# The second down-projection of a decoder trunk by seven block products

## The chip, the cores and the metric

The kernel runs on one core of one Trainium2 chip. The metric is the device time of one execution in microseconds; what is given as the time of the kernel is the median of several runs. Beside the runs there is one execution taken with the hardware profiler, and all rows below come from that one.

## The reference

The program is a decoder trunk of two layers on 1024 tokens of 1024 channels, in float32. The first layer mixes with a gated short convolution and differential attention, the second with RWKV-7 time mixing. After each mixer stands a channel mixer (FFN), and it is the second FFN that the change is about:

```python
def conv_glu_ffn(x, w_up, conv_w, conv_b, w_down):
    h = causal_dwconv(x @ w_up, conv_w) + conv_b
    gate, up = jnp.split(h, 2, axis=-1)
    return (jax.nn.silu(gate) * up) @ w_down
...
        f = conv_glu_ffn(x, ffn_w_up[l], ffn_conv_w[l], ffn_conv_b[l], ffn_w_down[l])
        x = layer_norm(DN_ALPHA * x + f, ln2_g[l], ln2_b[l])
```

The inner width is 2816, so `w_up` is 1024 x 5632 and `w_down` 2816 x 1024. The convolution reaches two tokens back.

## The kernel before

**Precision.** Every large product is made of three matmuls (`mm3`, lines 135 to 139): each operand is split into a rounded high part and the remainder in float32r, and high x high, high x low and low x high are summed in PSUM. `split` (line 113) makes the parts: a cast on ScalarE (L114) and a subtraction on VectorE (L115).

**The FFN.** `ffn` (line 215) is a generator that is called once for each layer `l`. The 2816 inner channels are `NC` = 22 chunks of 128. For each chunk `c` the up-projection makes a gate and a value tile, channels by 1024 tokens. Seven block products already stand in place of eight there (a Winograd form of Strassen's scheme): the 2 x 2 blocks are the gate and value weights by the two halves of the 1024 inputs, and the tokens' two halves. `block` (line 230) loads a chunk's weights with two transfers of 512 KB (`wr<-wup`, L236, on SP's queue) and makes the sums S1 to S4 on VectorE (L246). `cast` and `sub` (L254, L261) split a block five products ahead. From chunk 2 on, `chained` (line 358) emits one product of 12 matmuls (four input blocks by three passes) and then the other engines' work; the order of the products in a chunk is 1, 6, 2, 5, 7, 3, 4. Bank reads between products are `u` L366 and L376, `hv` L379 to L385 and `gi` L383. `late` (line 329) spreads the convolution, the gate and the loads of chunk `c` over the products of chunk `c + 1`: at product 1 it calls for S1 of the chunk after, at product 7 it multiplies gate and value (L353) and stores the tile in DRAM as `G` (L354, on POOL's queue).

**The down-projection.** `operands` (line 397) loads a chunk's half of `G` (256 KB, SP) and its 128 x 1024 rows of `wdn` (512 KB, SP) and splits both; `down` (line 421) multiplies them into PSUM. Tokens go in two groups of 512. In a group each of four token tiles has two banks (1024 output columns), and all 22 chunks are summed into them: 2 groups x 22 chunks x 4 token tiles x 2 column halves x 3 passes are 1056 matmuls. At the end of a group the last chunks (six in the last group) are taken one token tile at a time, so that adding the residual, the statistics, the normalization and the store of a tile run beside the matmuls of the next (`tail`, L489 to L498).

**Order.** The program is written in one sequence and a scheduler makes each engine's queue from it: an engine takes the first instruction in the text whose inputs and buffers are free. From chunk 2 on, the up-projection stands in a region (`manual_schedule`) in which the engines of `ORDERED`, that is TensorE, VectorE and ScalarE, keep the order of the text; SP, which issues the loads, and POOL are not among them. Buffers: `U` is a pool of 40 tiles of 512 KB, `W` of 6 and `RAW` of 2; a chunk's first weight tile is in `RAW`, its second in `U`. A load of the second FFN's weights is queued on SP behind the load of the next chunk's `RAW` tile, which waits for the sum S4 that last reads the tile before.

Of the kernel before, what the change touches and what calls it, by code (L numbers as in the profile page):

```python
# [16 lines left out]
P = 128  # L17
T = 1024
# [18 lines left out]
SUMS = 6  # L37
FIRST = (1, 2, 3, 5, 6, 7, 4)
# [22 lines left out]
class Kern:  # L61
# [153 lines left out]
    def ffn(self, l, xo, resid, row, tail, nxt=None):  # L215
# [7 lines left out]
        GS = [self.pd.tile([P, T], F32, name=f"G{l}_{c}") for c in range(NC)]  # L223
# [70 lines left out]
        def value(c):  # L294
            w = W[c]
            v = conv(w["h"], NC + c)
            nc.vector.tensor_tensor(v, w["g"], v, op=ALU.mult)
            nc.gpsimd.dma_start(GS[c], v)
            w.clear()
# [28 lines left out]
        def late(c, i):  # L328

            b = c - 1  # L330
            if i == 5 and c < NC:
                w = W[c]
                w["gi"] = self.U("gi")
                nc.scalar.copy(w["gi"][:, lo], w["x"])
            if i == 4:
                w = W[c]
                w["g"] = self.U("cv")
                tap(w["g"], w["gi"], c, 0)
            if b > 1:
# [46 lines left out]

        seq = [(c, i) for i in FIRST for c in range(2)]
# [15 lines left out]
        with ExitStack() as region:  # L403
            for n, (c, i) in enumerate(seq):
# [7 lines left out]
                if n == len(seq) - 3:  # L412
                    operands(0, 0)
                    operands(0, 1)
                yield
            for i in (1, 6, 2, 5, 7):
# [1141 lines left out]
def build(tc, ins, out, stop=None):  # L1558
    with ExitStack() as ctx:
# [18 lines left out]
        def mixed(i, l, w, resid, alpha, out_args, last_tail, nxt=None):  # L1578

            tail, res = k.make_tail(f"l{i}g", f"l{i}b", None, "hl")  # L1580
            gen = k.ffn(l, res["xo"], res["spill"], row(i), last_tail, nxt)
# [129 lines left out]
```

## Time and profile before

| | |
|---|---|
| median of 3 runs | 2765.36 us (2763.47 to 2773.1) |
| profiled execution, its own time | 2769.9 us |
| span of its instructions | 2768.1 us |
| TensorE matmuls, busy share of the span | 94% |
| VectorE | 70% |
| ScalarE | 41% |
| POOL (GpSimd) | 10% |
| mean granted TensorE clock | 0.958 of full speed |
| DMA | 358 MB, 129 GB/s in the mean |

A busy share is that of the engine's instructions over the span. Matmuls are pipelined: the profile gives 0.39 us to one, but they start 0.23 us apart, so costs are taken from counts over a stretch. An engine's idle time is listed with what ended it. The stages of interest: the first up-projection with its up matmuls from 533 to 971 us (the first of them between those of the mixer), the first down-projection to 1215, the second up-projection from 2081 to 2520, the second down-projection to 2758.

### The profile page before, as it was taken

Reading aid. Unit: us, or ns where it says so; the run is one execution under the profiler, and the core shown is the slowest. Engines: PE = TensorE matmul, PEld = TensorE weight load, DVE = VectorE, ACT = ScalarE, POOL = GpSimd, SP = SyncE. Lnnn points to the kernel's source line nnn. Section 1 sums busy time; section 2 is a strip of 40 time slices with the busy share of each in tenths; the row PEclk is TensorE's granted clock in tenths of the full one; section 3 lists DMA queues with packets and bytes.
Section 4 is the critical chain, followed back from the end, with each engine's and each line's share of the span. In section 5 each row is a group of like instructions: output and inputs, shape, how many; then the busy total and the mean of one; then the engine's idle time right before and its main releaser. Section 6 shows DMA issues by size and latency. Waiting matters only on the chain. (4 is left out here: it accounts for less than half of the span.)

```text
span 2768.1 us, 37639 instructions
## 1 busy us (share of the span) xinstructions
PE 2596.0 (94%) x14736; PEld 2133.1 (77%) x14736; DVE 1937.0 (70%) x3013; ACT 1123.2 (41%) x1706; POOL 275.4 (10%) x247
## 2 busy tenths in 40 slices
PE   8999989989999999999997988688898999999998
PEld 6777778778888888877876766677776888888887
DVE  4655655598888865667778656786758888887673
ACT  3333332344444441426676223333425444444330
POOL 0000000100000003010011011343420000000000
PEclk9999999999999999999998999887999999999999
DMA  5111223212222273633256678786441222225660
GB/s 168 54 46 44 73 88 110 85 61 92 76 84 92 73 264 117 218 128 114 91 183 236 221 219 234 182 195 171 174 147 46 94 82 92 76 84 184 230 217 31
DMA packets 208674, 358.07 MB, mean 129 GB/s; under 512 B 88944, under 2 KB 118256, under 8 KB 208496
## 3 DMA queue, kind: packets, MB, share of 16 engines
q1 hardware_dynamic: 198704, 320.01, 36.5%
q0 software_dynamic: 9792, 35.66, 3.4%
q8 instruction: 116, 1.90, 0.3%
q14 instruction: 62, 0.51, 0.1%
HBM read 255.46 MB, written 95.94 MB: 127 GB/s over the span
## 5 line engine op out<-in xcount | busy, mean ns | idle before, releaser
L137 PE MATMUL up<-x,wu 128*128 128x512 f32 x1232 | 481.8, 393 | 18.5 <-DVE u L312 8.2
L138 PE MATMUL up<-x,wu 128*128 128x512 f32 x1232 | 482.9, 392 | 0.3 <-DVE x L145 0.2
L139 PE MATMUL up<-x,wu 128*128 128x512 f32 x1232 | 482.0, 391 | 0.0
L137 PEld LDWEIGHTS up<-x,wu 128*128 128x128 f32 x1232 | 232.8, 189 | 71.0 <-ACT x L144 14.4
L138 PE MATMUL dn<-wdl,gt 128*128 128x512 f32 x704 | 273.7, 389 | 0.0
L137 PE MATMUL dn<-wdh,gt 128*128 128x512 f32 x704 | 272.2, 389 | 0.3 <-ACT xf L179 0.3
L139 PE MATMUL dn<-wdh,gt 128*128 128x512 f32 x704 | 272.3, 389 | 0.0
L138 PEld LDWEIGHTS up<-x,wu 128*128 128x128 f32 x1232 | 233.1, 189 | 50.7 <-DVE x L145 2.7
L139 PEld LDWEIGHTS up<-x,wu 128*128 128x128 f32 x1232 | 233.0, 189 | 48.7
L254 ACT CAST wu<-ws 128x512 fp32r<-128x512 f32 x176 | 109.3, 623 | 288.4 <-PE up L139 198.8
L137 PE MATMUL pr<-xv,wph 128*128 128x512 f32 x384 | 154.0, 405 | 9.7 <-DVE kp L1156 7.7
L137 PE MATMUL pj<-x,wih 128*128 128x512 f32 x384 | 153.1, 409 | 7.5 <-ACT x L144 7.5
L115 DVE TENSOR_TENSOR wdl<-raw,wdh 128x1024 fp32r<-128x1024 f32 x88 | 109.7, 1246 | 68.7 <-ACT wdh L114 55.5
L138 PE MATMUL pr<-xv,wph 128*128 128x512 f32 x384 | 153.9, 401 | 3.5 <-DVE xv L915 3.5
L139 PE MATMUL pr<-xv,wpl 128*128 128x512 f32 x384 | 154.2, 402 | 2.6 <-DVE wpl L115 2.6
L139 PE MATMUL pj<-x,wil 128*128 128x512 f32 x384 | 153.8, 401 | 0.2 <-DVE wil L115 0.2
L138 PE MATMUL pj<-x,wih 128*128 128x512 f32 x384 | 153.8, 400 | 0.0
L137 PEld LDWEIGHTS dn<-wdh,gt 128*128 128x128 f32 x704 | 132.2, 188 | 27.8 <-ACT xf L179 0.5
L138 PEld LDWEIGHTS dn<-wdl,gt 128*128 128x128 f32 x704 | 132.2, 188 | 27.7 <-DVE wdl L115 0.3
L139 PEld LDWEIGHTS dn<-wdh,gt 128*128 128x128 f32 x704 | 132.2, 188 | 27.3
L114 ACT CAST wdh<-raw 128x1024 fp32r<-128x1024 f32 x88 | 92.6, 1052 | 108.6 <-DMA raw<-wdn 103.5
L254 ACT CAST wu<-wr 128x512 fp32r<-128x512 f32 x132 | 81.4, 623 | 125.1 <-PE up L139 62.8
(319 smaller groups left out, 5230.8 us busy)
## 6 DMA issues: line engine op xcount, KB each, us to landing
wr<-wup SPq DMA_DIRECT2D x88, 512.0 KB, 4.2
raw<-wdn SPq DMA_DIRECT2D x88, 512.0 KB, 4.2
G<-cv POOLq DMA_DIRECT2D x44, 512.0 KB, 2.9
gr<-G SPq DMA_DIRECT2D x88, 256.0 KB, 4.1
bk<-bkS SPq DMA_DIRECT2D x32, 512.0 KB, 5.9
res<-spill SPq DMA_DIRECT2D x24, 512.0 KB, 4.6
raw<-win SPq DMA_DIRECT2D x22, 512.0 KB, 3.7
spill<-res SPq DMA_DIRECT2D x16, 512.0 KB, 2.8
```

What stands on the lines that cost most here:

```text
L114: self.nc.scalar.copy(hi, raw)
L115: self.nc.vector.tensor_sub(lo, raw, hi.bitcast(F32))
L137: nc.tensor.matmul(ps, ah, bh, start=first, stop=False, **kw)
L138: nc.tensor.matmul(ps, ah, bl, start=False, stop=False, **kw)
L139: nc.tensor.matmul(ps, al, bh, start=False, stop=last, **kw)
L254: nc.scalar.copy(t[:, lo], src)
```

## The change

The second down-projection (`fast`, layer 1 alone) becomes seven block products. With the even chunks and the odd chunks as the two halves of the inner dimension, the left operand A is `G` (token half by chunk parity) and the right operand B is `w_down` (chunk parity by column half). One term of such a product is a *slot*: one pair of chunks `m` (11 of them), 512 tokens by 512 columns, 12 matmuls. Seven products of 11 slots are 77 slots.

The sums of blocks are not made by an engine but by transfers that add to their target in DRAM (`accum_op`), which only POOL's queue issues. The weight sums T1 to T4 (`weight_sums`) are in the text of the first up-projection, at every odd chunk. The sums of `G`, S1 to S4, are made where a chunk is stored (`store`) in the second up-projection: 4 transfers for an even chunk, 7 for an odd one, in place of one each. [...] In the down-projection (`blocks`) SP loads the two operands of a slot (2 x 256 KB), both are split, and the products run in the order `DOWN` over three sets of four banks; residual, block adds, statistics and output are a list of small works, of which each slot takes a portion (`step`). The last chunk's convolution is put into the same list.

```diff
+DOWN = (1, 6, 2, 5, 3, 7, 4)
+WHEN = (4, 7, 10, 13, 18, 21, 24, 27)
...
-        GS = [self.pd.tile([P, T], F32, name=f"G{l}_{c}") for c in range(NC)]
+        fast = l == 1
...
+        def weight_sums(m):
+            t = self.TS[m]
+            b = {f"B{i}{j}": wdn[l + 1, 2 * m + i - 1, :, j * 512 - 512:j * 512] for i in (1, 2) for j in (1, 2)}
+            put = nc.gpsimd.dma_start
+            for n, x in (("T1", "B11"), ("T3", "B12"), ("T2", "B11"), ("T4", "B21")):
+                put(t[n], b[x])
+            for n, x in (("T1", b["B12"]), ("T3", b["B22"]), ("T2", t["T3"]), ("T4", t["T2"])):
+                put(t[n], x, accum_op=ALU.add, max_dma_last_dim=512)
+
+        def store(c, g, v):
+            if not fast:
+                nc.vector.tensor_tensor(v, g, v, op=ALU.mult)
+                nc.gpsimd.dma_start(GS[c], v)
+                return
+            s, put = SS[c // 2], nc.gpsimd.dma_start
+            for h in (lo, hi):
+                if (h is hi) == (c % 2 == 1):
+                    nc.vector.scalar_tensor_tensor(v[:, h], g[:, h], -1.0, v[:, h], ALU.mult, ALU.mult)
+                else:
+                    nc.vector.tensor_tensor(v[:, h], g[:, h], v[:, h], op=ALU.mult)
+            if c % 2 == 0:
+                put(s["S3"], v[:, hi])
+                put(s["N11"], v[:, lo])
+                put(s["S1"], v[:, hi])
+                put(s["S3"], v[:, lo], accum_op=ALU.add)
+            else:
+                put(s["S2"], v[:, hi])
+                put(s["S4"], v[:, lo])
+                put(s["A12"], v[:, lo])
+                put(s["N22"], v[:, hi])
+                put(s["S1"], v[:, hi], accum_op=ALU.add)
+                put(s["S2"], s["S3"], accum_op=ALU.add, max_dma_last_dim=512)
+                put(s["S4"], s["S2"], accum_op=ALU.add, max_dma_last_dim=512)
...
-                    nc.vector.tensor_tensor(w["v"], w["g"], w["v"], op=ALU.mult)
-                    nc.gpsimd.dma_start(GS[b], w["v"])
+                    store(b, w["g"], w["v"])
...
+        terms = {1: ("N11", "B11"), 6: ("S2", "T2"), 2: ("A12", "B21"), 5: ("S1", "T1"), 3: ("S4", "B22"), 7: ("S3", "T3"), 4: ("N22", "T4")}
+        slots = [(i, m) for i in DOWN for m in range(NC // 2)]
...
+        def bring(k):
+            i, m = slots[k]
+            a, b = terms[i]
+            t = raws[k] = self.W("dr", F32)
+            nc.sync.dma_start(t[:, lo], SS[m][a])
+            nc.sync.dma_start(t[:, hi], self.TS[m][b] if b[0] == "T" else wdn[l, 2 * m + int(b[1]) - 1, :, int(b[2]) * 512 - 512:int(b[2]) * 512])
...
+            def finished(i, t):
+                a, b = rs[t], rs[4 + t]
+                if i == 1:
+                    nc.scalar.copy(at(us, t), X[t])
+                elif i == 6:
+                    later(put, at(u2, t), at(us, t), Y[t], front=True)
+                elif i == 2:
+                    later(put, a[:, lo], a[:, lo], X[t], ALU.subtract)
...
+                elif i == 4:
+                    put(b[:, lo], b[:, lo], Z[t], ALU.subtract)
+                    halves(4 + t, 0)
+                    norm(4 + t)
+                    for v in (lo, hi):
+                        later(out, 4 + t, v, cost=1.4, after=1)
...
+            def step():
+                n = tick[0]
+                tick[0] += 1
+                ahead = 5 if n < 6 * 11 - 8 else 9
+                for _ in range(2):
+                    if ready[1] < min(len(slots), n + 1 + ahead):
+                        if ready[0] <= ready[1]:
+                            bring(ready[0])
+                            ready[0] += 1
+                        split_slot(ready[1])
+                        ready[1] += 1
+                    if n < 4:
+                        break
+                while ready[0] < min(len(slots), ready[1] + 3):
+                    bring(ready[0])
+                    ready[0] += 1
...
+            for p, i in enumerate(DOWN):
...
+                ps = X if i in (1, 2) else Z if i in (7, 4) else Y
+                n = NC // 2
+                first = 3 if i in (3, 4) else 1
+                last = 7 if i == 4 else 3 if i in (5, 7) else 1
+                groups = [range(first)] + [range(m, m + 1) for m in range(first, n - last)] + [range(n - last, n)]
+                for g in groups:
+                    for t in range(4):
+                        for m in g:
+                            h, w = parts[p * n + m]
+                            tk = slice(t * P, t * P + P)
+                            self.mm3(ps[t], h[:, tk], w[:, tk], h[:, hi], w[:, hi], m == 0 and i in (1, 6, 7), m == n - 1, skip_group_check=True)
+                            mms[0] += 3
+                            if mms[0] % 12 == 0:
+                                step()
+                        if g[-1] == n - 1:
+                            finished(i, t)
...
+                if n > 14 and i == 3 and not fast:
+                    for m in (0, 1) if c == 3 else (c // 2,) if c % 2 else ():
+                        weight_sums(m)
+                if fast:
+                    if n >= len(seq) - 4:
+                        bring(n - len(seq) + 4)
+                    if n >= len(seq) - 2:
+                        split_slot(n - len(seq) + 2)
+                elif n == len(seq) - 3:
```

## Rows read from the trace of the kernel before

**Rows 1.** Windows: stretch, its length, busy us (instructions) by engine, clock, DMA share, GB/s

```profile
600.00:800.00 200.00, 200.00 (x884) 165.58 (x883) 166.33 (x223) 92.47 (x126) 6.64 (x12) 1.00 0.25 88
...
2200.00:2400.00 200.00, 199.06 (x878) 164.22 (x877) 166.26 (x221) 91.75 (x126) 5.33 (x10) 1.00 0.22 79
...
2500.00:2600.00 100.00, 100.00 (x443) 82.84 (x442) 69.31 (x74) 45.07 (x57) 3.16 (x4) 1.00 0.69 236
```

**Rows 2.** Tiles `up` and `dn`: duration ns min/median/max, first and last start in us

```profile
L139 PE MATMUL up<-x,wu x1232: 387/389/632, 534.0 to 2519.8; 128*128 128x512 f32 x176
...
L139 PE MATMUL dn<-wdh,gt x704: 388/389/397, 971.5 to 2758.3; 128*128 128x512 f32 x176
```

**Rows 3.** Waits, 2150 to 2520 us: us in total, times, longest

```profile
DVE ws L246 <- DMA wr<-wup: 32.5, 18, 3.3
...
PE up L137 <- DVE u L376: 0.9, 2, 0.8
```

**Rows 4.** Timeline of the second up-projection: start, us, instruction [idle before <-releaser]

```profile
2229.51 0.69 DVE L383 TENSOR_TENSOR gi<-u,up 128x512 f32<-128x512 f32 x1 [0.75 <-PE up L139]
2236.30 0.69 DVE L246 TENSOR_TENSOR ws<-wr 128x512 f32<-128x512 f32 x1 [1.58 <-DMA wr<-wup]
2248.55 0.69 DVE L383 TENSOR_TENSOR gi<-u,up 128x512 f32<-128x512 f32 x1 [0.82 <-PE up L139]
2256.42 0.69 DVE L246 TENSOR_TENSOR ws<-wr 128x512 f32<-128x512 f32 x1 [2.66 <-DMA wr<-wup]
2259.56 0.50 PE L137 MATMUL up<-x,wu 128*128 128x512 f32 x1 [0.17 <-DVE u L376]
```

**Rows 5.** DMA in 2229.5:2237 (40 slices; queue: packets, MB, share), then 2248.5:2256.5

```profile
DMA  6000000000000004977985899798989820000000
...
q1 hardware_dynamic: 288, 1.05, 41.0%
...
q1 hardware_dynamic: 288, 1.05, 41.4%
...
q8 instruction: 1, 0.02, 0.9%
```

**Rows 6.** Groups by line, 2500 to 2768 us: shapes, count, busy us, mean ns

```profile
L115 DVE TENSOR_TENSOR wdl<-raw,wdh 128x1024 fp32r<-128x1024 f32 x44 | 53.8, 1223 | 36.6 <-ACT wdh L114 28.7 <-issue 3.6 <-PE dn L138 2.9
L471 DVE TENSOR_TENSOR res<-res,dn 128x512 f32<-128x512 f32 x16 | 10.9, 683 | 45.1 <-PE dn L139 45.1
L496 DVE SCALAR_TENSOR_TENSOR res<-res,mv,bc 128x512 f32<-128x512 f32 x16 | 11.2, 744 | 0.0
...
L114 ACT CAST wdh<-raw 128x1024 fp32r<-128x1024 f32 x44 | 46.3, 1052 | 53.0 <-DMA raw<-wdn 51.1 <-PE dn L138 1.7
```

**Rows 7.** Timeline of POOL's issues in the second layer

```profile
1789.51 0.76 POOL L1467 DMA_DIRECT2D gt<-gateS  x1
...
2246.21 0.53 POOL L354 DMA_DIRECT2D G<-cv  x1 [18.42 <-DVE cv L353]
```

**Rows 8.** DMA of the span: queue 0; issues with KB each and median us to landing

```profile
q0 software_dynamic: 9792, 35.66, 3.4%
...
G<-cv POOLq DMA_DIRECT2D x44, 512.0 KB, 2.9
...
raw<-xT SPq DMA_DIRECT2D x8, 512.0 KB, 3.5
```

**Rows 9.** Timeline of POOL and of SP's queue at the start

```profile
0.73 0.53 POOL L1254 MEMSET ST<- 128x512 f32 x1 [0.29 <-POOLq L1704]
...
5.54 0.33 SPq L878 DMA_DIRECT2D msk<-msk  x1
```

**Rows 10.** Windows of the start, and TensorE's longest wait in 0 to 140 us

```profile
0.00:30.00 30.00, 22.47 (x86) 18.33 (x87) 13.89 (x30) 13.45 (x21) 0.94 (x6) 1.00 0.70 232
30.00:70.00 40.00, 34.70 (x156) 27.18 (x156) 21.16 (x33) 14.01 (x27) 0.00 (x0) 0.98 0.43 117
...
PE pj L137 <- ACT x L144: 7.5, 1, 7.5
```

More of the change, by code (lines that the diff above doesn't have):

```diff
@@ L212, in mixer_operands, with ffn @@
                 put(name, ts[j][:, d])
-    def ffn(self, l, xo, resid, row, tail, nxt=None):
+    def ffn(self, l, xo, resid, row, tail, nxt=None, out_row=None):
         nc = self.nc
@@ L222, in ffn @@
         lo, hi = slice(0, 512), slice(512, 1024)
-        GS = [self.pd.tile([P, T], F32, name=f"G{l}_{c}") for c in range(NC)]
+        fast = l == 1
+        GS = [] if fast else [self.pd.tile([P, T], F32, name=f"G{l}_{c}") for c in range(NC)]
+        dram = lambda names: [{n: self.pd.tile([P, 512], F32, name=self.nm(n)) for n in names} for _ in range(NC // 2)]
+        SS = dram(("N11", "A12", "N22", "S1", "S2", "S3", "S4")) if fast else []
+        if not fast:
+            self.TS = dram(("T1", "T2", "T3", "T4"))
+        def weight_sums(m):
[7 more added lines that the diff above has]
+        def store(c, g, v):
+            if not fast:
+                nc.vector.tensor_tensor(v, g, v, op=ALU.mult)
[20 more added lines that the diff above has]
+                put(s["S4"], s["S2"], accum_op=ALU.add, max_dma_last_dim=512)
         W = [{} for _ in range(NC)]
@@ L295, in value @@
             w = W[c]
-            v = conv(w["h"], NC + c)
-            nc.vector.tensor_tensor(v, w["g"], v, op=ALU.mult)
-            nc.gpsimd.dma_start(GS[c], v)
+            store(c, w["g"], conv(w["h"], NC + c))
             w.clear()
@@ L385, in chained @@
                 add(w["h"][:, lo], w["u"][:, hi], ps)
+        terms = {1: ("N11", "B11"), 6: ("S2", "T2"), 2: ("A12", "B21"), 5: ("S1", "T1"), 3: ("S4", "B22"), 7: ("S3", "T3"), 4: ("N22", "T4")}
+        slots = [(i, m) for i in DOWN for m in range(NC // 2)]
+        raws, parts = {}, {}
+        def bring(k):
[4 more added lines that the diff above has]
+            nc.sync.dma_start(t[:, hi], self.TS[m][b] if b[0] == "T" else wdn[l, 2 * m + int(b[1]) - 1, :, int(b[2]) * 512 - 512:int(b[2]) * 512])
@@ new lines, in split_slot @@
+        def split_slot(k):
+            t = raws.pop(k)
+            h, w = self.U("dh", F32R), self.U("dl", F32R)
+            parts[k] = h, w
+            if slots[k][0] in (2, 6):
+                nc.scalar.activation(h[:, lo], t[:, lo], AF.Copy, scale=-1.0)
+                nc.scalar.copy(h[:, hi], t[:, hi])
+                nc.vector.scalar_tensor_tensor(w[:, lo], t[:, lo], -1.0, h[:, lo].bitcast(F32), ALU.mult, ALU.subtract)
+                nc.vector.tensor_sub(w[:, hi], t[:, hi], h[:, hi].bitcast(F32))
+            else:
+                self.split(t, h, w)
@@ L411, in ffn @@
                     chained(n, c, i)
-                if n == len(seq) - 3:
+                if n > 14 and i == 3 and not fast:
[7 more added lines that the diff above has]
+                elif n == len(seq) - 3:
                     operands(0, 0)
@@ L415, in ffn @@
                 yield
+            if fast:
+                blocks()
+                return
             for i in (1, 6, 2, 5, 7):
@@ L1580, in mixed @@
             tail, res = k.make_tail(f"l{i}g", f"l{i}b", None, "hl")
-            gen = k.ffn(l, res["xo"], res["spill"], row(i), last_tail, nxt)
+            gen = k.ffn(l, res["xo"], res["spill"], row(i), last_tail, nxt, row(3))
             res["fill"] = lambda n: drain(gen, n)
```

70 lines of the change are left out of this document (added).

## The prediction

> **What bounds the kernel now.** I read the busy shares by stretch first [rows 1]. In both up-projections and in the first part of the second down-projection TensorE is busy 199.1 to 200.0 us of 200 and 100.0 of 100, at full granted clock. A change there is worth what it takes off TensorE or adds to its waits. The row from 2500 to 2600 holds 443 matmuls in 100 us, so one costs 0.2257 us. The rows of the tiles `up` and `dn` [rows 2] place the stage: the last up matmul starts at 2519.8, the last down matmul at 2758.3, 1056 matmuls in 238.5 us, 0.2258 each. Down matmuls run back to back.
>
> Then I looked for what is nearly late in the second up-projection, since the change puts transfers there. The waits of that stretch [rows 3] show VectorE waiting 18 times, 32.5 us in all, for `wr<-wup`, one chunk's weight load, at the block sum L246; TensorE waits only twice, 0.9 us in all. So the load is late for VectorE in nearly every chunk, but seldom for TensorE. The reader sees how near in the timeline of VectorE [rows 4]. Count from the start of `gi` L383, when product 3 is done. In the ordinary chunk L246 starts 6.79 us later (2229.51 to 2236.30). In a late one (2248.55 to 2256.42) it is 7.87, and there TensorE waits, 0.17 us, for the add `u` L376 that stands behind L246 on VectorE. So the load may land about 7.7 after `gi`; the slack is 0.9 us, once a chunk, and beyond it each microsecond goes to TensorE. What made the late one late is in the DMA queues of the two windows [rows 5]: the same 288 packets of the load, but one instruction fetch beside them, 0.9% of 16 engines over 8.0 us, 1.15 us of a single engine. One busy engine spends the slack.
>
> **What is removed.** Seven products of 11 block pairs, 4 token tiles and 3 passes are 924 matmuls in place of 1056. 132 x 0.2257 = 29.8 us, if the operands keep up.
>
> **What the down-projection adds.** A slot is 12 matmuls, 2.71 us. VectorE: 77 splits of 1.22 us, 94; eight residual tiles of two operations as wide as a split, 20; 36 block adds and 16 statistics of 512 columns, 0.68 each, 35; 16 output halves of two operations of 0.74, 24; means, and the last chunk's taps, about 13 [rows 6]. That is 186 of 208.5 us, a cover of 22 us. The adds that TensorE waits for (a bank of product 5 or 7 read before 3 or 4 writes it) have 27 matmuls of the other token tiles, 6.1 us, before them, and the splits run five, later nine slots ahead; I cost these at nothing. If the cover is gone, a bank costs its 0.68 us four times at each of two turns, 5 us. ScalarE has 77 casts of 1.05, 81 us, and hides. DMA: 77 slots of 2 x 256 KB, 8 residuals, 4 MB out and the broadcast rows are 51 MB in 208 us, 243 GB/s, against 236 at a share of 0.69 while TensorE was full [rows 1]. The end is the same chain: add, statistics, two output halves, store. I take 0.5 us for the first split and for a half output still queued; bounds 0 and 3.
>
> **What the second up-projection adds.** Per pair of chunks POOL issues 11 transfers of 256 KB in place of 2 of 512. A POOL issue takes 0.53 to 0.76 us [rows 7]: 11 are some 7 us of 38, plus waits for landings of about 2.9 us each [rows 8] at the accumulates; POOL hides. In VectorE's `store` two halves of 0.68 replace one product of 1.22; the stage has VectorE at 83%. The queue is what matters. Queue 0 took 3.4% of 16 x 2768.1 us for 35.66 MB [rows 8]: 0.69 us on each engine for a plain 256 KB. No accumulate is in the trace. Below, it costs a plain one, 0.69; above I take three times, 2.07; I take twice, 1.38. (The Trainium skill, "DMA: Bandwidth & Descriptors", section "Rules for kernel authors", says that an accumulate reads its destination and writes it later. Estimated from that, three movements for two make 1.04 us; the odd chunks below would then cost 1.3 us and the time would be 2745.)
>
> Place them. The store of a chunk is issued 2.3 us before `gi` (POOL at 2246.21, `gi` at 2248.55), and the weight loads fill +2.8 to +6.4, the busy slices of the window that begins with `gi` [rows 4, 5, 7]. For an even chunk three plain writes are through by +1 and one accumulate, which waits for a landing, ends before +3.3: hidden; uncovered it would cost up to 2.07 - 0.9 in 9 chunks, 11 us. For an odd chunk four plain writes end near +1.4, then come S1 and S2, 2.8 us of accumulates, and one of the two falls among the loads: 1.38 - 0.9 = 0.5 us in 9 chunks, 4 us. S4 waits for S2 to land and comes after the loads. Bounds: 0 (both through before) and 2 x 2.07 - 0.9 = 3.2 in 9 chunks, 29.
>
> **Where the weight sums go.** The text puts 88 transfers (four copies, four accumulates, 11 times) into the first up-projection. They wait for nothing but one another. The rows at the start [rows 9] show what the program does with such work on POOL and SP: the memset of `ST`, line 1254, and the load of `msk`, line 878, belong to the odd layer's mixer, whose code is reached after the first down-projection, yet they run at 0.73 and 5.54 us. Only TensorE, VectorE and ScalarE are held to the written order. So I expect the 88 at the start of the kernel, not at 600 to 960 us, and the first up-projection untouched. POOL needs at least 88 x 0.55 = 48 us to issue them, and the engines 44 x 0.69 + 44 x 1.38 = 91 us. In the first 30 us the loads already take a DMA share of 0.70, in the next 40 of 0.43, with TensorE's first matmul waiting 7.5 us for x [rows 10]. If queue 0 gets one 2 KB packet for each of the loads' 4 KB, half their bytes, the loads' 21 busy us of the first 30 become 31.5; TensorE has idle time and a little lead there, and I take 8 us for the whole start. Bounds: 0 (they fit between), and 21, if byte goes for byte. Later the loads are fewer (a DMA share of 0.25 in the first up-projection, [rows 1]) and I let them hide.
>
> **The sum.** The profiled execution took 2769.9 us (span 2768.1 and 1.8 around it). 2769.9 - 29.8 + 0.5 + 4 + 8 = 2752.6. The median of the three shown lies 4.5 below that execution: 2748, down 0.6%.
>
> **The rivals.**
> *All hidden.* An accumulate is as cheap as a plain write, and the start absorbs the 88: 2769.9 - 29.8 + 0.5 - 4.5 = 2736. For it: DMA shares of 0.22 and 0.25 in the up-projections [rows 1]. Against: the slack of 0.9 us, and the crowded first 30 us.
> *Dearer accumulates.* At three times a plain write one and a half of them fall among the loads of an odd chunk, 3.1 - 0.9 = 2.2 in 9, 20 us, and the start costs 12: 2769.9 - 29.8 + 0.5 + 20 + 12 - 4.5 = 2768, nothing won. For it: one fetch of 1.15 us already broke the slack [rows 5].
> *Slower: every weight load is met.* Place: the 18 loads of [rows 3]. If the accumulates run on from chunk to chunk, each load meets one and a half of them, 2.2 us past the slack in 18 chunks, 40 us: 2769.9 - 29.8 + 0.5 + 8 + 40 - 4.5 = 2784. It decides from (29.8 - 8.5) / 18 = 1.2 us past the slack in every chunk. Against it: POOL is idle 18.4 us before each store now [rows 7], and should end each store inside its own chunk. (The Trainium skill, same page, section "Issuing engines are not separate DMA queues", states that transfers from different engines share the same 16 DMA engines and interleave, so a queue of its own protects no load; this rival is that rule at full price.)
> That the 88 stay in the first up-projection would put 1 to 3 us on some 9 loads there and free the start: the same sum within its range.
>
> **Chances.** About 0.5%, 14 us, is what a measurement here can tell from no change: faster is below 2751.5, slower above 2779. The forecast has 0.40, with its own range 2742 to 2756; 0.28 of that below 2751.5. All hidden 0.20 (2733 to 2742), dearer accumulates 0.27 (2756 to 2778), every load met 0.13. Faster 0.48, same 0.39, slower 0.13. The range 2734 to 2777 leaves out the last rival and the edge of the first.
>
> **What will show it.** 924 down matmuls in about 209 us with no TensorE wait inside: the removed term. L246 still waiting once a chunk, by 6.8 us after `gi` in the chunks of an even store and 8 to 9 in the others, with a TensorE wait at the adds of product 6 (`u`) of 0.3 to 0.7 us in the latter: the second term. Queue 0 busy from the first microseconds, and the first x and weight loads landing later than 3.5 us: the third. Wrong would be: matmuls of the down-projection waiting for splits or for a block sum that has not landed (POOL late at the turn of the stages); accumulates under 1 us or over 2 of engine time; queue 0 busy at 600 to 960 us instead; or another order of SP's loads, which would take the slack itself away or double it.

## The result, and the profile after

The changed kernel takes 2797.98 us, median of four runs (2792.92 to 2809.13), against 2767.03 us for the kernel before on the same chip: ratio 1.0113, 95% interval 1.0085 to 1.0142, 31 us slower. The forecast was 2748 us, its range 2734 to 2777. The profiled execution took 2809.13 us (span 2807.4).

The first and last matmuls of the tiles `up` and `dn` cut the span into stages. This table, in us, has the kernel before, the changed kernel and all experiments of the sections below; "between" is from the last down matmul of the first layer to the first up matmul of the second, which is the time mixing, and the second down-projection counts from the last up matmul.

| kernel | first `up` | 1st up-proj. | between | 2nd up-proj. | 2nd down-proj. | span |
|---|---|---|---|---|---|---|
| before | 533.1 | 438.3 | 865.8 | 439.4 | 238.5 | 2768.1 |
| changed | 562.7 | 438.0 | 860.7 | 467.8 | 225.8 | 2807.4 |
| e1_no_weight_sums | 533.5 | 439.3 | 861.3 | 459.9 | 229.0 | 2774.9 |
| e3_plain_store | 564.8 | 438.0 | 858.4 | 438.7 | 222.6 | 2777.6 |
| e4_down_alone | 530.7 | 437.5 | 864.9 | 437.8 | 224.2 | 2748.1 |
| e6_rows_2k | 568.5 | 438.0 | 860.1 | 460.5 | 225.0 | 2805.9 |
| e2_sums_held | 533.9 | 460.6 | 881.5 | 459.6 | 227.3 | 2814.9 |
| e5_early_load | 565.6 | 437.5 | 865.1 | 436.8 | 226.2 | 2783.5 |
| e7_down_order | 564.2 | 437.5 | 861.1 | 464.1 | 222.3 | 2801.6 |
| e8_all | 534.7 | 456.2 | 873.6 | 436.6 | 225.5 | 2779.8 |
| e9_half_order | 565.0 | 437.5 | 861.3 | 460.4 | 217.3 | 2794.6 |
| e10_held_all | 544.3 | 438.2 | 868.8 | 436.6 | 214.2 | 2756.2 |
| e11_before_early | 534.8 | 437.6 | 871.7 | 437.7 | 238.5 | 2773.3 |
| e13_all_mid | 553.0 | 438.7 | 867.5 | 436.4 | 213.9 | 2762.5 |
| e14_held_product3 | 535.1 | 438.3 | 862.2 | 437.0 | 213.6 | 2740.2 |
| e15_copies_only | 560.0 | 438.7 | 871.0 | 458.9 | 223.5 | 2804.0 |

Three stages moved. The start is 29.6 us later, the second up-projection 28.4 us longer, the second down-projection 12.7 us shorter where 29.8 were hoped for; the stretch between is 5.1 us shorter, less than the 10 us by which it varies among the kernels e1, e4, e11 and e14 (861.3 to 871.7), which keep the order of the kernel before there. The profiled execution is the slowest of the four: in five other kernels with the same store and loads the second up-projection takes 458.9 to 464.1 us. Its granted clock over that stage is 0.97, against 0.99 before and in e9; that is some 8 of the 28.4 us, estimated from the two clocks. With 460 there, the terms are 29.6 + 21 - 13 - 5 = 33, near the 31 of the medians.

**The start.** The windows of the changed kernel:

```profile
0.00:30.00 30.00, 10.60 (x29) 7.54 (x30) 8.15 (x21) 7.93 (x12) 16.01 (x30) 0.87 0.95 302
30.00:70.00 40.00, 31.91 (x121) 23.02 (x119) 10.54 (x14) 10.92 (x18) 21.64 (x26) 0.93 1.19 299
70.00:130.00 60.00, 54.03 (x226) 41.86 (x227) 37.58 (x67) 18.49 (x39) 38.68 (x40) 0.86 1.33 238
```

Its longest TensorE wait in 0 to 560 us, POOL's first transfers in the timeline, and the DMA view of 0 to 150 us (columns as in [rows 8]):

```profile
PE pj L139 <- ACT x L146: 24.6, 7, 9.2
```

```profile
1.25 4.35 POOL L238 DMA_DIRECT2D T<-wdn  x8 [0.81 <-POOLq L1910]
```

```profile
q0 software_dynamic: 26752, 23.07, 83.7%
...
raw<-xT SPq DMA_DIRECT2D x8, 512.0 KB, 8.5
```

As predicted, the weight sums' copies (L238) are issued from 1.25 us on and not in the first up-projection. But beside [rows 10] TensorE makes 29 matmuls in the first 30 us and not 86; it waits 24.6 us for x in place of 7.5, because a load of x lands after 8.5 us and not 3.5 ([rows 8]).

**The second up-projection.** Waits of 2115 to 2573 us, to be held against [rows 3], and the timeline of one odd chunk with its store on POOL, against [rows 4]:

```profile
DVE ws L289 <- DMA wr<-wup: 61.3, 17, 5.8
PE up L139 <- DVE u L416: 19.4, 16, 3.3
```

```profile
2263.39 0.69 DVE L423 TENSOR_TENSOR gi<-u,up 128x512 f32<-128x512 f32 x1 [0.19 <-PE up L141]
2263.45 0.93 POOL L264 DMA_DIRECT2D S<-cv  x1
2272.08 0.69 DVE L289 TENSOR_TENSOR ws<-wr 128x512 f32<-128x512 f32 x1 [3.49 <-DMA wr<-wup]
2274.05 1.01 POOL L266 DMA_DIRECT2D S<-S  x1 [7.38 <-DMA S<-S]
```

The block sum now starts 8.69 us after `gi` (2263.39 to 2272.08), where [rows 4] had 6.79 and a limit of about 7.7, and TensorE meets the same add of product 6 late in 16 chunks instead of 2. An even chunk is no better, 8.76 us; its accumulate (L258) waits for the landing of the write before it and is issued 1.6 us before SP issues the loads, in five others only 0.4 us before:

```profile
2242.96 0.69 DVE L423 TENSOR_TENSOR gi<-u,up 128x512 f32<-128x512 f32 x1 [0.83 <-PE up L141]
2243.35 0.89 POOL L258 DMA_DIRECT2D S<-cv  x1 [1.88 <-DMA S<-cv]
2244.93 0.88 SPq L279 DMA_DIRECT2D wr<-wup  x2
2251.72 0.69 DVE L289 TENSOR_TENSOR ws<-wr 128x512 f32<-128x512 f32 x1 [3.55 <-DMA wr<-wup]
```

**The second down-projection.** TensorE's waits from 2573 us on, the timelines of PE and VectorE at two of them, and one window:

```profile
PE dn L139 <- DVE res L466: 7.0, 4, 3.4
PE dn L139 <- ACT u L492: 2.3, 2, 1.6
PE dn L140 <- DVE dl L448: 1.8, 1, 1.8
```

```profile
2751.19 0.39 PE L141 MATMUL dn<-dh,dl 128*128 128x512 f32 x1
2751.63 1.22 DVE L117 TENSOR_TENSOR dl<-dr,dh 128x1024 fp32r<-128x1024 f32 x1
2752.76 0.74 DVE L484 SCALAR_TENSOR_TENSOR res<-res,mv,bc 128x512 f32<-128x512 f32 x1
2753.54 0.75 DVE L485 SCALAR_TENSOR_TENSOR res<-res,rstd,bc 128x512 f32<-128x512 f32 x1
2754.21 0.68 DVE L466 TENSOR_TENSOR res<-res,dn 128x512 f32<-128x512 f32 x1
2754.94 0.50 PE L139 MATMUL dn<-dh 128*128 128x512 f32 x1 [3.37 <-DVE res L466]
...
2781.88 0.39 PE L141 MATMUL dn<-dh,dl 128*128 128x512 f32 x1
2782.30 0.69 DVE L466 TENSOR_TENSOR res<-res,dn 128x512 f32<-128x512 f32 x1 [10.39 <-PE dn L141]
2783.04 0.50 PE L139 MATMUL dn<-dh 128*128 128x512 f32 x1 [0.78 <-DVE res L466]
```

```profile
2752.00:2767.00 15.00, 10.29 (x30) 7.83 (x31) 12.36 (x18) 3.14 (x3) 0.92 (x1) 0.77 0.26 99
```

The 924 matmuls are there, but four times TensorE stops until a block add (L466) has read a bank. Counted in matmuls of the stage, the stops of products 7 and 4 come before the first matmul of token tiles 1 and 3 of the product's last group, and the two waits for `u` (a bank read by ScalarE, L492) at the same tiles of product 1. Tiles 0 and 1, and 2 and 3, are the two halves of one two-bank tile of PSUM. What TensorE waits for there is a semaphore, so this order stands in the program; what the chip would do without it no run here shows. At 2782.30 the read is in time and the stop is the read itself; at 2754.21 it stands behind a split and two output operations on VectorE's queue, and the stop is 3.37 us. Behind that stop and the next the clock falls: the granted clock of the window is 0.77, some 7 us of it at the lower level of 1.2 GHz, and matmuls start 0.43 us apart.

### The profile page after: what moved, and what is told of

The parts are those of the page before. It is cut to its first block, busy times and chain, and to the rows that moved or that the text cites. A ratio compares the mean times of both kernels' runs of the same rounds, so it can differ in the third digit from the quotient of the medians.

```text
span 2807.4 us, 37862 instructions
## 1 busy us (share of the span) xinstructions
PE 2580.4 (92%) x14604; PEld 2106.6 (75%) x14604; DVE 1967.1 (70%) x3066; ACT 1137.5 (41%) x1721; POOL 427.0 (15%) x434
## 5 line engine op out<-in xcount | busy, mean ns | idle before, releaser
L139 PE MATMUL up<-x,wu 128*128 128x512 f32 x1232 | 486.6, 397 | 36.6 <-DVE u L416 19.4
L139 PE MATMUL pj<-x,wih 128*128 128x512 f32 x384 | 155.1, 415 | 26.3 <-ACT x L146 24.6
L140 PE MATMUL dn<-wdl,gt 128*128 128x512 f32 x352 | 136.9, 389 | 0.2 <-DVE rstd L162 0.2
L139 PE MATMUL dn<-wdh,gt 128*128 128x512 f32 x352 | 136.3, 390 | 0.3 <-ACT xf L181 0.3
L141 PE MATMUL dn<-wdh,gt 128*128 128x512 f32 x352 | 136.2, 389 | 0.0
L139 PE MATMUL dn<-dh 128*128 128x512 f32 x308 | 121.8, 396 | 9.3 <-DVE res L466 7.0
L304 DVE TENSOR_TENSOR wu<-ws,wu 128x512 fp32r<-128x512 f32 x176 | 120.4, 684 | 4.0 <-ACT wu L297 4.0
L140 PE MATMUL dn<-dl,dh 128*128 128x512 f32 x308 | 121.2, 393 | 1.8 <-DVE dl L448 1.8
L141 PE MATMUL dn<-dh,dl 128*128 128x512 f32 x308 | 121.2, 393 | 0.0
L316 DVE SCALAR_TENSOR_TENSOR cv<-hv,par,cv 128x1023 f32<-128x1023 f32 (+1 forms) x88 | 113.1, 1285 | 0.1
```

What stands on the lines that cost most here:

```text
L139: nc.tensor.matmul(ps, ah, bh, start=first, stop=False, **kw)
L140: nc.tensor.matmul(ps, ah, bl, start=False, stop=False, **kw)
L141: nc.tensor.matmul(ps, al, bh, start=False, stop=last, **kw)
L304: nc.vector.tensor_sub(t[:, hi], src, t[:, lo].bitcast(F32))
L316: nc.vector.scalar_tensor_tensor(cc[:, k:], src[:, :T - k], self.pc_(wname, 88 - 44 * k + ct), cc[:, k:], ALU.mult, ALU.add)
```

## The experiments

The theories: **A**, the weight sums at the start take the DMA engines from the first loads. **B1**, the accumulates make the up weights land after VectorE wants them, and nothing else; **B2**, eleven transfers in place of two do that, whatever their kind. **C**, the down-projection's stops are VectorE's backlog; **D**, found on the way, they come from the two halves of a PSUM tile.

**e1_no_weight_sums.** The call of the weight sums is left out, and the second down-projection reads plain blocks of the weight in their place.

```diff
...
-                if n > 14 and i == 3 and not fast:
+                if False:
```

> Left out: the eleven times four weight sums T1 to T4 (their 88 transfers are not issued, and the second down-projection reads plain blocks of the weight of the same size in their place). Theory A (the hoisted sums share the DMA engines with the first loads): the first up-projection begins at about 533 us again instead of 562.7, PE waits for x about 7.5 us in the start instead of 24.6, and the time falls by 30 us to about 2768. Rival (the late start is a side effect of another order of instructions, the transfers themselves are cheap): the first up-projection still begins after 555 us and the time stays within 8 us of 2798. The second up-projection (467.5 us) and the second down-projection (226 us) should not move by more than 4 us.

Measured: 2777.37 us, ratio to before 1.0032 (1.0017 to 1.0047). The first up-projection begins at 533.5 us, as A has it. (The time is 9 us above the expected 2768, probably because the 30 us were the profiled execution's and were taken from the median, which is 11 us lower.) The windows of its start:

```profile
0.00:30.00 30.00, 22.47 (x87) 18.30 (x87) 13.88 (x30) 13.47 (x21) 1.00 (x6) 1.00 0.69 231
30.00:70.00 40.00, 35.01 (x159) 27.70 (x158) 21.90 (x35) 14.54 (x28) 0.00 (x0) 0.98 0.39 118
70.00:130.00 60.00, 60.00 (x271) 47.26 (x271) 37.23 (x63) 19.30 (x37) 0.00 (x0) 0.93 0.19 57
```

By 130 us TensorE has made 87 + 159 + 271 = 517 matmuls here and 29 + 121 + 226 = 376 in the changed kernel: 141 x 0.2257 = 32 us of work, the size of the loss. 96 of them, 22 us, are lost by 70 us, the rest later.

Leaving out the call also gives the engines and SP the order of the kernel before again, so this run alone does not tell the transfers from the order, the rival. SP's queue does, for most of the loss: its first 22 issues are the same in the kernel before and in the changed one, the eight loads of x among them, and the load that follows these eight is issued at

```profile
25.73 0.33 SPq L119 DMA_DIRECT2D raw<-win  x1
```

before and, since the loads of x are longer on their way, at

```profile
47.33 0.33 SPq L121 DMA_DIRECT2D raw<-win  x1
```

in the changed kernel, 21.6 us later. For the 10 us lost from 70 to 130 us the order remains a rival.

**e3_plain_store.** The accumulates of `store` become plain transfers.

```diff
-                put(s["S3"], v[:, lo], accum_op=ALU.add)
+                put(s["S3"], v[:, lo])
...
-                put(s["S4"], s["S2"], accum_op=ALU.add, max_dma_last_dim=512)
+                put(s["S4"], s["S2"])
```

> Left out: the additions in the block sums of the activations. Every accumulating transfer of the store becomes a plain one of the same source, destination and place in the queue, so that the number of transfers and their order stay. Theory B1 (the accumulates' price, 1.42 and 2.08 us of each engine, delays the weight loads): VectorE's wait for the up weights falls from 61 us to between 35 and 45, the second up-projection from 467.5 us to about 445 to 452, the time to about 2776 to 2783. Theory B2 (eleven transfers in place of two for each pair of chunks are enough, whatever their kind): the second up-projection stays above 460 us, the time above 2790. The start stays at 562.7 us in both.

Measured: 2781.69 us, ratio 1.0050 (1.0033 to 1.0067). The second up-projection takes 438.7 us, all of the loss back and more than expected. Waits of 2115 to 2544 us:

```profile
DVE ws L289 <- DMA wr<-wup: 36.2, 17, 3.1
...
PE up L139 <- DVE u L416: 0.6, 1, 0.6
```

VectorE waits as in [rows 3] and TensorE hardly at all. It is the adding, not the number of transfers; B2 falls. (The edit also takes the short rows from the transfers between DRAM tiles; e6 shows that rows of 2048 bytes alone give nothing.)

**e4_down_alone.** No sums at all and the store of the kernel before; only the seven products, on blocks of the same size, are left of the change.

```diff
...
-                nc.sync.dma_start(t[:, lo], SS[m][a])
+                nc.sync.dma_start(t[:, lo], GS[2 * m + (a != "N11")][:, hi if a == "N22" else lo])
...
```

> Left out: all sums outside the TensorE products. The gated chunks are stored as in the kernel before, one plain transfer each; no weight sum and no activation sum is made; the seven products read blocks of the stored chunks and of the weight, of the right size and number. What is left of the change is the second down-projection by seven products. Theory (start, store and down-projection are three separate losses and gains): the start is back at 533 us (-30), the second up-projection back at 439 us (-28), the down-projection stays at about 226 us because its 17 us of loss are VectorE's and the late residual loads' own; time about 2740. Rival (the down-projection's loss comes from transfers still under way and from loads behind them): the down-projection also falls, to 212 to 216 us, and the time to about 2728.

Measured: 2750.07 us, ratio 0.9927 (0.9907 to 0.9947). The start and the up-projection are back, and the down-projection still takes 224.2 us, with the same 7.1 us of waits for `res`. So its loss is its own, and the three terms are separate. The time is 10 us above the expected 2740, probably for the same reason as in e1.

**e6_rows_2k.** The accumulates between DRAM tiles in longer rows.

```diff
-                put(t[n], x, accum_op=ALU.add, max_dma_last_dim=512)
+                put(t[n], x, accum_op=ALU.add, max_dma_last_dim=2048)
```

> Nothing left out: the accumulating transfers between DRAM tiles go in rows of 2048 bytes in place of 512. Theory (a packet's price is mostly fixed, 65 ns for 512 bytes, and 2048 bytes cost the 178 ns that the accumulates from SBUF show): an accumulate takes 8 x 178 ns = 1.42 us of each engine in place of 2.08; the start's transfers take about 92 us of the engines in place of 121, so the first up-projection begins at 550 to 556 us in place of 562.7, the second up-projection shortens by 4 to 10 us, time about 2780 to 2788. Rival (the price goes by bytes, so that such a packet takes 4 x 65 = 260 ns): nothing moves by more than 3 us, time about 2797.

Measured: 2805.07 us, ratio 1.0132 (1.0112 to 1.0152): no gain, as the rival says, but not for its reason. The DMA view of 0 to 150 us:

```profile
q0 software_dynamic: 9856, 23.07, 66.1%
...
raw<-xT SPq DMA_DIRECT2D x8, 512.0 KB, 10.2
```

The same bytes take the queue 66.1% in place of 83.7%, so the price did fall; and the start is 568.5 us, not earlier. Its second up-projection, 460.5 us, lies within what kernels with short rows show, so the cheaper accumulates gave nothing there either. What the start loses was therefore open, and e15 takes it up.

**e2_sums_held.** POOL keeps the order of the text in the first FFN.

```diff
-manual_schedule(engines=ORDERED)
+manual_schedule(engines=ORDERED if fast else ORDERED | {mybir.EngineType.Pool})
```

> Nothing left out: POOL too keeps the order of the text within the first layer's FFN, so that the 88 weight-sum transfers are issued during the first up-projection, behind the stores of their chunks, and not at the kernel's start. Theory A (the start loses what the first microseconds' transfers take from the first loads): the first up-projection begins at 533 us, -30. What it costs the first up-projection is bounded by the sums' spell: if its weight loads, which land late by the same few us as in the second up-projection, are met by VectorE, it takes up to 20 us more than 438; if they have slack there, under 5. I expect 5 to 10, time 2773 to 2778. Rival (the sums cost 30 us wherever they stand): time 2798 +- 6.

Measured: 2811.40 us, ratio 1.0146 (1.0118 to 1.0173). The start is 533.9 us, but the first up-projection takes 460.6, 22 more, past the 20 that I gave as the bound. Waits of 534 to 994 us:

```profile
DVE ws L289 <- DMA wr<-wup: 55.0, 18, 7.3
...
PE up L139 <- DVE u L416: 17.2, 10, 4.8
```

It is the second up-projection's loss, line for line, at the place to which the sums were moved. Another 21 us are lost between, in the time mixing, where in the stretch from 1778 us ScalarE waits once 16.5 us for a load of `wo`; the scheduler had put the instructions there in another order. (e8 has that order and, once, a wait of 16.4 us, but 873.6 us between, so the order is at most a part of the 21.)

**e5_early_load.** The second weight half asked for earlier, in the second up-projection alone.

```diff
+            fast and i == 7 and c + 2 < NC and block(c + 2, "early")
```

(`block` then makes only the load of the second half, and later only that of the first.)

> Nothing left out: the second half of each chunk's up weights in the second up-projection is asked for at product 7 of two chunks before, and no longer first at product 1 of the chunk before, where it stands on SP's queue behind the first half of the next chunk's weights. All accumulating transfers stay. Theory B1 (an accumulate costs the second up-projection only by making the weight load land after VectorE wants it): VectorE's wait for wr falls from 61 us to under 15, the second up-projection from 467.8 us to 435 to 444, the time to about 2768 to 2774. Rival B3 (the accumulates also hold up something else: POOL's issue, the store's tiles, the clock): it stays above 455 us and the wait moves to another line.

Measured: 2784.86 us, ratio 1.0043 (1.0021 to 1.0065). The second up-projection takes 436.8 us; no wait of VectorE's L289 for `wr` is left. From 2200 to 2400 us, with every accumulate of the stretch in it, TensorE is busy 200.00 us.

B1 holds and B3 falls. The median is above the expected 2774, since the start and the stretch between were 3 and 4 us longer than in the changed kernel.

**e7_down_order.** Residual loads four steps earlier, and little other work in a step with two splits (`was` is `ready[1]` at the start of the step).

```diff
...
+                if n + 4 in WHEN:
+                    fetch(WHEN.index(n + 4))
...
+                left = (1.3, 1.3, 0.1)[ready[1] - was]; n in WHEN and residual(WHEN.index(n))
```

> Nothing left out: in the second down-projection each residual load is issued four steps earlier, and a step that splits two operands takes next to none of VectorE's queued work. Theory C (the 7 us of PE waits for res and the 3 to 4 us at half clock behind them come from VectorE's queue alone, filled by late residuals and by double splits): PE's wait for res falls from 7 us to 1 to 3, the down-projection from 225.8 us to 214 to 219, time 2787 to 2792. Rival (VectorE is short of time over the whole stretch, so that the wait goes elsewhere): the down-projection stays above 222 us.

Measured: 2802.85 us, ratio 1.0111 (1.0079 to 1.0142); down-projection 222.3 us, 3.5 less than the changed kernel and outside C's 214 to 219. The waits for late residuals are gone, TensorE's are not:

```profile
PE dn L139 <- DVE res L466: 5.4, 4, 1.9
PE dn L139 <- ACT u L492: 4.1, 2, 3.4
```

C explains the longest stop for `res` (3.4 to 1.9 us), not the stops' number and place, and their sum is no smaller: one for `u` has grown to 3.4 us, and 9.5 us stand for 9.3. What is won is the 1.8 us of the split's wait and half of the slow stretch (granted clock 0.89 from 2748 to 2763 us, where the changed kernel had 0.77 in as long a window). That led to D.

**e8_all.** The edits of e2, e5, e6 and e7 together.

> Nothing left out: sums held back into the first up-projection, early loads, the down-projection's new order, and 2048-byte rows in the accumulates, together. By A, B1 and C the gains add up: -22 (start, less what the first up-projection pays), -26 (second up-projection), -8 to -10 (down-projection), so 2738 to 2745, 1% faster than the kernel before. Rival (the transfers find another place to hurt): above 2755.

Measured: 2786.50 us, ratio 1.0048 (1.0033 to 1.0064); the rival. Start and second up-projection are as good as expected (534.7, 436.6), but the first up-projection keeps its loss (456.2), the time mixing takes 873.6 and the down-projection 225.5 us.

**e9_half_order.** Token tiles in the order 0, 2, 1, 3.

```diff
-                    for t in range(4):
+                    for t in (0, 2, 1, 3):
...
-                last = 7 if i == 4 else 3 if i in (5, 7) else 1
+                last = 7 if i == 4 else 3 if i in (5, 7, 1) else 1
```

> Nothing left out: in the second down-projection the four token tiles of a group of products are taken in the order 0, 2, 1, 3, and product 1 too ends with a group of three operands; the rest is the changed kernel. The gaps of PE in the down-projection stand at the first matmul of tiles 1 and 3 of the last group of products 1, 7 and 4, where the tile before has just been finished into the other half of the same two-bank PSUM tile. Theory D (a matmul into one half waits for the read of the other half that was issued just before it): these gaps go, with the clock's drops behind them, PE's waits for res and u fall from 9.3 us to under 2, and the down-projection falls from 225.8 to 212 to 215 us, time 2784 to 2788. Rival C (VectorE's queue is late as such): the gaps only move to tiles 2 or to the next product, the down-projection stays above 220 us.

Measured: 2796.29 us, ratio 1.0092 (1.0063 to 1.0120); down-projection 217.3 us, 8.5 less.

```profile
PE dn L139 <- DVE res L466: 4.5, 4, 1.6
```

The two waits for `u` and both stops in the last group of product 4 are gone, which C doesn't explain. Four stops of 0.7 to 1.6 us stay: two before tiles 1 and 3 of product 7, and two before tiles 0 and 2 of product 4's first group, the move to the next product that rival C names; so it is 2 us past the expected range. D holds, with a part of C: together (e10, e13, e14) the two edits give 213.6 to 214.2 us, 5 to 6 above 924 x 0.2257.

The changed kernel has a control of D in itself. Product 5 ends like product 7, with a group of three and an add at once, but its four token tiles stand in four one-bank tiles of PSUM. Tile 1's first matmul there starts before tile 0 is read, without a wait:

```profile
2691.58 0.39 PE L139 MATMUL dn<-dh 128*128 128x512 f32 x1
2691.78 0.69 DVE L466 TENSOR_TENSOR res<-res,dn 128x512 f32<-128x512 f32 x1 [8.82 <-PE dn L141]
```

**e10_held_all.** All edits: sums held, after product 5; early loads in both up-projections; 2048-byte rows; e7 and e9.

> Nothing left out: the weight sums held in the first up-projection (after product 5), early loads in both up-projections, 2048-byte rows, the residual loads' and splits' new order and the tile order 0, 2, 1, 3. By A, B1 and D: start 534 us, first up-projection 437 to 442 (it was 456 to 461 with the sums and without early loads), second 437, down-projection 212 to 214. The stretch between, 861 us in the changed kernel, was 874 and 882 us in the two runs that held POOL's order; at 861 to 882 the sum gives 2735 to 2757. Rival (with the sums in it the first up-projection is bound by the transfers themselves): it stays above 450 us, time above 2755.

Measured: 2750.36 us, ratio 0.9930 (0.9907 to 0.9953), as expected. With early loads the first up-projection carries the sums in 438.2 us. Only the start is 544.3 and not 534. Its DMA view of 0 to 150 us has the likely reason:

```profile
T<-wdn POOLq DMA_DIRECT2D x12, 256.0 KB, 6.5
...
T<-T POOLq DMA_DIRECT2D x4, 256.0 KB, 4.5
```

Two of the eleven groups of sums, 16 transfers, are still issued at the start, from 1.25 us on. After product 5 of chunk 3 they stand in the text ahead of the store at product 7, so keeping POOL's order gave them nothing to wait behind. The first up-projection carries nine groups here; e14 has all eleven there.

**e11_before_early.** The control: early loads in the kernel before.

> Nothing left out: the kernel before with the early loads in both up-projections and nothing else, as a control of what the early loads are worth without the change. The second up-projection of the kernel before loses 3 us to the late loads (439.4 us; 436.8 with accumulates and early loads), the first about 1 us: time 2760 to 2765, within 0.3% of before. Rival (the early loads are a gain of their own, of 10 us and more): below 2757.

Measured: 2770.16 us, ratio 1.0006 (0.9991 to 1.0021). The early loads are worth nothing without the change. (It is above the expected 2765, with 871.7 us between.)

**e13_all_mid.** The edits of e6, e7 and e9, early loads in the second up-projection alone, and each copy of the sums made to follow the attention's first store; POOL is not held. Of the edit, the last part:

```diff
...
+                put(t[n][0:1, 0:128], self.hold[0:1, 0:128]); put(t[n], b[x])
```

> Nothing left out: as the run with all four edits, but the weight sums are neither at the start nor in the first up-projection: each of their plain copies is made to follow the first store of the attention's channels at about 125 us, and early loads are kept for the second up-projection alone. Theory A (the sums hurt where the kernel needs its loads at once, as in the first 30 us): the first up-projection begins at 533 to 545 us, the first up-projection keeps its 438 us, the rest as in the run before: time 2735 to 2750. Rival (121 us of transfers cost the attention as much as the start): the first up-projection begins after 555 us, time above 2755.

Measured: 2760.74 us, ratio 0.9964 (0.9948 to 0.9979). The first up-projection begins at 553.0 us, later than theory A had it; the sums cost the attention too, or its other order does, and this run can't tell the two apart. (The matmuls are lost from 70 to 300 us, 974 in place of 1079, and the DMA share is 0.89 from 130 to 200 us, where the kernel before has 0.11; that speaks for the sums.)

**e14_held_product3.** As e10, the sums after product 3.

> Nothing left out: as the run with all edits and the sums held in the first up-projection, but the sums stand after product 3 of a chunk as in the text of the changed kernel, and not after product 5; that gives the attention the same order of VectorE's, ScalarE's and SP's instructions as in the run that held the sums and did nothing else. Theory A (the start is 534 us whenever no sums run in it; the 544 us of the run after product 5 came from its other order in the attention): first up-projection begins at 534 us, the rest as there (438, 244, 869, 437, 214, 10): time 2736 to 2746. Rival (the early loads in the first up-projection or the held sums themselves cost the attention 10 us): it begins at 544 us, time about 2750.

Measured: 2740.77 us against 2764.15 for the kernel before, ratio 0.9918 (0.9891 to 0.9945), 23 us faster. Its windows of the up-projections and TensorE's wait in the down-projection:

```profile
600.00:800.00 200.00, 200.00 (x883) 165.50 (x883) 168.49 (x223) 91.44 (x126) 39.57 (x60) 1.00 0.58 152
2200.00:2400.00 200.00, 200.00 (x884) 165.62 (x883) 168.52 (x232) 90.79 (x125) 38.19 (x59) 1.00 0.48 130
```

```profile
PE dn L139 <- DVE res L466: 3.0, 3, 1.5
```

The start is 535.1 us, as theory A has it, with all sums in the first up-projection and none at the start. That the 10 us of e10 came from another order of the attention's instructions is not shown: e10 had 16 of the 88 transfers at the start, and they are the likelier cause (TensorE makes 66 matmuls there in the first 30 us, and 89 here). TensorE is full in both up-projections [rows 1] with every transfer of the change in them.

**e15_copies_only.** The 44 accumulates of the weight sums are left out.

> Left out: the 44 accumulating transfers of the weight sums, so that T1 to T4 are plain blocks; the 44 plain copies stay at the kernel's start, with the rest of the changed kernel. Theory A1 (the start loses to the first copies, which fill the DMA engines with 11.5 MB while the first loads are awaited, so that cheaper accumulates changed nothing): the first up-projection still begins after 553 us, time above 2786. Theory A2 (the accumulates' engine time, 92 of 121 us, is the loss): it begins before 543 us, time below 2780.

Measured: one run, 2805.81 us; the first up-projection begins at 560.0 us. The DMA view of 0 to 150 us:

```profile
q0 software_dynamic: 3520, 11.54, 22.8%
...
raw<-xT SPq DMA_DIRECT2D x8, 512.0 KB, 9.3
```

A1 holds for the start: the copies alone delay x as much as everything did. The 44 copies went in packets of 4 KB, as the loads do. (The time stays above 2786 as well, but 10 us of that is a longer stretch between.) The run gives the accumulates' price too. Of 16 x 150 us of the engines, 83.7 - 22.8% for 44 accumulates on 16 engines are 2.08 us on each engine for one in 512-byte rows, and with e6's 66.1%, 1.48 us in 2048-byte rows; a plain copy here is 0.78. (An accumulate from SBUF, as `store` has it for S1 and S3, has 2 KB packets, 204 ns each in the second up-projection of the changed kernel: 1.6 us.)

## Why the prediction was wrong

**The removed matmuls** were right: 924, 0.2257 us apart, and no wait for a load.

**The turn and the tail, 0.5 us.** This step failed. "The adds that TensorE waits for ... have 27 matmuls of the other token tiles, 6.1 us, before them ... I cost these at nothing" looked at single banks and at the next product alone. TensorE stops at the read of the other half of the same two-bank tile, inside the same product, with no matmul between. In the changed kernel 9.3 us of waits for `res` and `u`, 1.8 for a split, and about 3 us of slower clock behind them; the other 3 of the 17 us stand in no single wait. e9 and product 5 show the place, e7 what VectorE's backlog adds to one stop. My price for a lost cover, 5 us, named the wrong turn.

**The second up-projection, 4 us.** The slack of 0.9 us and the waits that would follow were right (L289, then the add of product 6), and e5 shows that it is the only path. The step that failed is the overlap in the even chunks: the one accumulate, which I had through before the loads, is mostly issued 0.4 to 1.6 us ahead of them and falls among them. In the median of 18 chunks L289 starts 8.6 us after `gi`, where the kernel before has 6.9, in even chunks as in odd ones. The 1.7 us between are about one accumulate from SBUF, 1.6 us and not the 1.38 that I took: 0.9 past the limit in 18 chunks and not 0.5 in 9. TensorE shows it as 19.4 us of waits, and the stage loses 20 to 28 us. The accumulates between DRAM tiles, 2.08 us and as dear as my upper bound, do not count here: with 1.48 (e6) the median is the same 8.6. The rival "every weight load is met" (0.13, 40 us) is what happened in this stage at half of its price, though not because the accumulates run on from chunk to chunk: the last one of the odd chunk is issued at 2274.05, after the load has landed. (The Trainium skill, "DMA: Bandwidth & Descriptors", section "Issuing engines are not separate DMA queues": transfers that the gpsimd and the sync engine start run on the same 16 DMA engines and interleave. The traces agree, 8.7 us against 6.8. The estimate that I made from its section "Rules for kernel authors", 1.04 us for an accumulate, is below all that was measured, 1.48 to 2.08.)

**The start, 8 us.** The hoisting was predicted rightly; the size failed. The upper bound, 21 us, let the loads of the first 30 us be doubled; by 70 us 22 us were indeed lost, and it went on to 130 us, to 29.6. I had taken 8 because the queue would give the loads two packets' bytes of three; in fact a load of x took 8.5 us for 3.5, and the copies' packets were as large as the loads', which is the "byte for byte" of my upper bound. The accumulates' price, on which I had spent the care, doesn't matter there (e6, e15).

**The sum.** 2748, with 21 more for the start, 17 for the up-projection and 16 for the down-projection, less 5 for the mixing, is 2797. That it meets the median to 1 us rests on taking 460 for the up-projection and is partly luck. Only the up-projection stayed within my bounds (29); the start, 29.6, went past its 21, and the down-projection's 17 far past its 3. No rival let all three be dear together. What stays open: why the stretch between runs from 858 to 882 us, of which 861 to 872 with one and the same order of instructions; what of the start's last 10 us is order; and what of e13's start is due to the sums.

## What to carry to other kernels

Work that waits for nothing is put where its engine is free, which can be the kernel's first microseconds; ask for its text to be held where the loads have slack, behind something that waits (e10 had nothing there), and make that slack first. A load that is late by a microsecond once a chunk is cured by asking for it earlier, not by cheaper neighbours: with early loads the same transfers cost nothing. Where a product finishes tile by tile, finish the halves of one PSUM tile apart from one another, and count the reads inside the product, not only at its end.

## What the runs showed of the hardware that was not expected

An accumulate between DRAM tiles cost 2.08 us of each DMA engine for 256 KB in 512-byte rows and 1.48 in 2048-byte rows, where a plain copy cost 0.78; one from SBUF cost 1.6. An even chunk's store, with one accumulate from SBUF, made the block sum that waits for a load of 2 x 512 KB start 1.7 us later in the median; cheaper accumulates between DRAM tiles made no difference to that (e6). 11.5 MB of plain copies at the start made a 512 KB load land after 9.3 us in place of 3.5, and adding 11.5 MB of accumulates behind them made it no later (8.5).
